# Feed-forward down products kept in PSUM: six banks that accumulate over all groups for the first 384 tokens, five rotating banks for the other 768

## The chip, the cores and the metric

The kernel runs on one core of a Trainium2 chip. The metric is device time in microseconds (us) of one execution. TensorE (PE) does the matrix products, VectorE (DVE), ScalarE (ACT) and GpSimd (POOL) the elementwise work, and SyncE (SP) issues the DMAs. Results of TensorE land in PSUM, which has eight banks of 128 partitions x 512 float32 values; DVE and ACT read it, POOL does not here.

## The reference

One layer of a hybrid backbone: 1024 sample tokens and 128 prompt tokens (nine tiles of 128) go through a mixer (mLSTM and attention), and then through a feed-forward part. The change touches the feed-forward part alone:

```
D_MODEL = 1024; D_FF = 4096; DEPTH = 1; ALPHA = 2 ** 0.25
x = layer_norm(ALPHA * x + g1 * mix, ln1_g, ln1_b)
h = x * (1 + sc2) + sh2
ff = jnp.square(jax.nn.relu(h @ w_up)) @ w_down
x = layer_norm(ALPHA * x + g2 * ff, ln2_g, ln2_b)
```

All of it is float32. The kernel splits each operand of a product in a high and a low part and takes three products (high x high, high x low, low x high): the helper `mm3`, lines 78 to 80.

## The kernel before

The 4096 hidden features are worked through in 16 groups (`NFB`) of 256. For each group there is an *up* product, the activation, and a *down* product that adds to the output of every token. The tokens are in two parts.

**First part, T0: tiles 0, 1, 2 (384 tokens).** `up_plain(fb)` loads two weight slots of `w_up` (`w_pair`: DMA to a `raw` buffer, high part on ACT in line 72, low part on DVE in line 73), runs 2 x 24 matmuls of 384 columns into banks of tag `u`, and takes relu (ACT), square (DVE) and the split to `ah`, `al`. `down(..., [fb], ...)` then does for three token tiles and two halves of 512 columns six matmuls into a bank of tag `d`, and DVE evicts it: a copy into `acc0` for group 0 (line 1168), an add to `acc0` for the later groups (line 1170). Groups 14 and 15 go together, twelve matmuls into one bank, and their eviction is part of the output stage: times gate `g2`, plus `acc0`, statistics of the layer norm (lines 1173 to 1175), then `finish` (lines 1139 to 1150). Before that, `residual` (lines 1131 to 1137) has multiplied `acc0` by the gate on POOL and has added ALPHA times the residual stream, read back from `x1d`.

While T0 runs, `act_forms` (lines 1112 to 1128) makes sums and differences of the activations of the other tokens: 32 operations on POOL, 16 additions and 16 subtractions, each subtraction followed by a split on ACT and DVE. The last of the nine token tiles is modulated and transposed late, between the two halves of `up_plain(1)` (`last_mod`, `modulate2`); the transposes use a pool of two banks, `ps3t`.

**Second part, T1: tiles 3 to 8 (768 tokens).** `up_halves` makes the up product with seven block products in place of eight (a Strassen-like scheme): 84 matmuls of 384 columns into three banks x, y and z. Its weights are sums of blocks, made by `up_forms` (POOL for the sums, line 1281, ACT and DVE for the splits) into three rotating `uf` slots. `down` runs twelve bank fills of six matmuls per group, each evicted by DVE.

PSUM before: pool `ps4` has three banks of tag `u` and three of tag `d`; `psx` has one bank each for x and y; z is taken from `u`.

The text of the kernel gives each operation a place, but the build orders the queue of each engine by planned times of its own, so an operation can stand ahead of ones that come earlier in the text.

Of the kernel before, what the change touches and what calls it, by code (L numbers as in the profile page):

```python
# [9 lines left out]
F32 = mybir.dt.float32  # L10
F32R = mybir.dt.float32r
# [25 lines left out]
def hybrid_step_kernel(  # L37
# [27 lines left out]
    def load(out, in_):  # L65
        nc.sync.dma_start(out=out, in_=in_)
# [892 lines left out]


    st3r = ctx.enter_context(ExitStack())
    st3 = ctx.enter_context(ExitStack())
    ps3t = pool(st3r, "ps3t", 2, space=PSUM, side="right")
    dp = pool(st3r, "dp", 1, side="right")
    ps3 = pool(st3, "ps3", 4, space=PSUM)
    xw = pool(st3, "xw", 4)
# [94 lines left out]

    x1s = {}

    def modulate2(s):
        if s // 3 not in h2T:
            h2T[s // 3] = t_alloc()
        hf = dt_([128, KT, 128], "m", 8)
        modulate(hf, s, x1s[s], sc2p, 24, t3)
# [32 lines left out]


    st4 = ctx.enter_context(ExitStack())
    ps4 = pool(st4, "ps4", 3, space=PSUM)
    tf = pool(st4, "tf", 1)
    fs = pool(st4, "fs", 1)
    wdv = kview(w_down)
    acts = {}
    for nm in ("s2", "s3", "a22"):
        acts[nm] = tuple(tf.tile([128, 4, TB], F32R, tag=nm + e, name="tf" + nm + e) for e in "hl")  # L1110

    def act_forms(mk):
        acts["a11"] = tuple(t[:, 0:4, :] for t in h2T[1])
# [41 lines left out]
    def down(mk, acc, toks, fbs, parts, ws, g2, l2, split_last):  # L1155
# [3 lines left out]
        for i, s in enumerate(toks):  # L1159
# [2 lines left out]
                st = mk([128, 2, 6], "bst", 2)  # L1162
            for half in range(2):
                cs = slice(512 * half, 512 * half + 512)
                g = ps4.tile([128, 512], F32, tag="d", name="d4")
                mm3(g[:], [((a[0][:, m, ts_], a[1][:, m, ts_]), (w[0][:, 0, cs], w[1][:, 0, cs])) for a, m, w in ws])
                if fbs[0] == 0:
                    nc.vector.tensor_copy(out=acc[:, i, cs], in_=g[:])
                elif not last:
                    nc.vector.tensor_tensor(out=acc[:, i, cs], in0=acc[:, i, cs], in1=g[:], op=ALU.add)  # L1170
                else:
                    tm = mk([128, 512], "x", 2)
                    nc.vector.tensor_tensor(out=tm[:], in0=g[:], in1=g2[0 if s < NS else 1][:, cs], op=ALU.mult)
                    nc.vector.tensor_tensor(out=acc[:, i, cs], in0=acc[:, i, cs], in1=tm[:], op=ALU.add)
                    nc.vector.bn_stats(out=st[:, half, :], in_=acc[:, i, cs])
# [36 lines left out]
            modulate2(late_.pop())  # L1212

    a = up_plain(0, lambda: None)
    nxt = up_plain(1, last_mod)
    st3r.close()
    s4r = ctx.enter_context(ExitStack())
    psx = pool(s4r, "psx", 1, space=PSUM, side="right")
    s4b = ctx.enter_context(ExitStack())
    ar0 = pool(s4b, "ar0", 1, side="right")  # L1220
    acc0 = ar0.tile([128, 3, D], F32, name="acc0")
    s4t = ctx.enter_context(ExitStack())
    tt4 = pool(s4t, "tt4", 1, side="right")
    forms = act_forms(lambda shape, tag: tt4.tile(list(shape), F32, tag=tag, name=tag))
# [2 lines left out]
        next(forms, None)  # L1227
        next(forms, None)

    T0 = (0, 1, 2)  # L1230
    for fb in range(NFB - 3):
        down(fat, acc0, T0, [fb], [a], down_w([fb]), None, None, False)
        a, nxt = nxt, up_plain(fb + 2, some_forms)
    for _ in forms:
        pass
# [10 lines left out]
    load_l2((l2a[:, 0, :], l2a[:, 1, :]))  # L1246
    todo = list(T0)

    def some():
        for _ in range(2):  # L1250
            if todo:
                s = todo.pop(0)
                residual(fft, acc0[:, s, :], s, g2a[:])

    down(fat, acc0, T0, [NFB - 3], [a], down_w([NFB - 3]), None, None, False)
    a, nxt = nxt, up_plain(NFB - 1, some)


    wuv = kview(w_up)
# [6 lines left out]
    def up_forms(fb):  # L1266
        raw = []
        for kh in range(2):
            t = rp.tile([128, 1024], F32, tag="raw", name="raw")[:].rearrange("p (k n) -> p k n", n=256)
            load(t, wuv[:, 4 * kh:4 * kh + 4, 256 * fb:256 * fb + 256])  # L1270
            raw.append(t)
        a11, a21 = raw[0][:, :, 0:128], raw[0][:, :, 128:256]
        a12, a22 = raw[1][:, :, 0:128], raw[1][:, :, 128:256]
        if fb:
            tmp = [wp.tile([128, 1024], F32R, tag="w" + e, name="wt" + e)[:] for e in "hl"]
        else:
            tmp = [fft([128, 1024], "wt", 2, F32R)[:] for e in range(2)]
# [26 lines left out]
        gen = up_forms(fb)  # L1304
        return gen, [next(gen) for _ in range(3)]

    ws = down_w([NFB - 2, NFB - 1])
    pre = up_begin(0)
    down(fft, acc0, T0, [NFB - 2, NFB - 1], [a, nxt], ws, [g2a], (l2a[:, 0, :], l2a[:, 1, :]), False)
    s4f.close()  # L1310
    s4b.close()
    s4a.close()
    fp = pool(st4, "fp", 1)
    aa = [fp.tile([128, 2, 768], F32R, tag="aa" + e, name="aa" + e) for e in "hl"]
    aa = ((aa[0][:], aa[1][:]), (ab[:, 0:2, :], ab[:, 2:4, :]))
    ar = pool(s4r, "ar", 1, side="right")
    acc = ar.tile([128, 6, D], F32, name="acc")

    def ft(shape, tag, bufs=1, ty=F32):
# [10 lines left out]
    def up_halves(pre, a, each):  # L1330
# [123 lines left out]
```

## Time and profile before

| | |
|---|---|
| time, median of 3 runs (lowest to highest) | 2518.7 us (2515.26 to 2519.15) |
| profiled execution, its own time | 2508.51 us |
| its span, first to last instruction | 2506.7 us |
| mean granted clock of TensorE, of full speed | 0.983 |
| TensorE busy | 2377.3 us, 95% of the span |
| DVE / ACT / POOL busy | 1553.9 / 991.4 / 489.4 us |
| T0 with the late token tile | about 1649 to 1945 us of the span |
| T1 | about 1945 to 2507 us |

The profiled execution took 2508.51 us, 1.8 us more than its span and 10.2 us less than the median of the three timed runs. A busy engine here is one with an instruction in progress; matmuls overlap, so the pace of TensorE is read from the starts of its instructions and not from their durations.

### The profile page before, as it was taken

The page shows a single profiled execution, that of the slowest core. Times are in us where ns is not written, and L with a number is a line of the kernel's source. Part 1 is how long each engine was busy: PE and PEld are TensorE (multiplying, and loading weights), DVE is VectorE, ACT ScalarE, POOL GpSimd, SP SyncE. Part 2 cuts the span into 40 slices and gives each one's busy share as a digit, 9 for nine tenths or more (in the row PEclk, how much of TensorE's full clock was granted, in tenths as well). Part 3 has the DMA queues.
Part 4 walks back from the last instruction along what each step waited for, and adds up shares of the span by engine and source line. Part 5 has one row for each costly group of instructions (what it writes and reads, how often), then busy time and mean ns, then how long its engine had stood idle before and what let it go on. Part 6 is the DMA issues. An engine that isn't in the chain of part 4 may idle for free.

```text
span 2506.7 us, 36075 instructions
## 1 busy us (share of the span) xinstructions
PE 2377.3 (95%) x13293; PEld 2136.6 (85%) x13293; DVE 1553.9 (62%) x2785; ACT 991.4 (40%) x2100; POOL 489.4 (20%) x635
## 2 busy tenths in 40 slices
PE   7999999999999899899999999997999899999996
PEld 4878887788999899889999999886998788888875
DVE  5645636646654554487885255777666766666678
ACT  3323423435433233276665242233333444433332
POOL 1001101102110010244441000343002422221143
PEclk9999999999999999999999999998999999999998
DMA  8275456445655643310004464233343221211223
GB/s 267 83 204 156 146 116 200 138 136 138 193 162 148 192 144 81 87 64 16 16 16 164 163 188 163 105 125 121 124 135 126 101 68 59 68 62 65 68 76 110
DMA packets 234544, 300.46 MB, mean 120 GB/s; under 512 B 24992, under 2 KB 175600, under 8 KB 234368
## 3 DMA queue, kind: packets, MB, share of 16 engines
q1 hardware_dynamic: 234368, 298.16, 38.7%
q8 instruction: 105, 1.72, 0.3%
q14 instruction: 71, 0.58, 0.1%
HBM read 232.88 MB, written 65.21 MB: 119 GB/s over the span
## 4 chain that ended last, share of the span: by engine, by line
PE 71%; DMA 9%; DVE 9%; POOL 4%; ACT 3%; issue 2%; SPq 0%; DVEq 0%; ACTq 0%; POOLq 0%
PE g L78 12%; PE g L80 12%; PE g L79 12%; PE d L78 3%; PE d L79 3%; PE d L80 3%; PE psy L1350 3%; PE t L872 2%; DMA raw<-in_w_down_dram 2%; DMA raw<-in_w_up_dram 2%; PE u L78 2%; PE u L79 2%; PE u L80 2%; POOL wth L1281 1%; DVE wl L73 1%
## 5 line engine op out<-in xcount | busy, mean ns | idle before, releaser
L78 PE MATMUL g<-th,wh 128*128 128x384 f32 x1088 | 373.2, 343 | 7.4 <-DVE fm L248 7.4
L80 PE MATMUL g<-th,wl 128*128 128x384 f32 x1088 | 367.7, 338 | 0.0
L79 PE MATMUL g<-tl,wh 128*128 128x384 f32 x1088 | 366.1, 337 | 0.0
L72 ACT ACTIVATE wh<-raw 128x1024 fp32r<-128x1024 f32 x180 | 188.8, 1058 | 258.9 <-DMA raw<-in_w_down_dram 87.3
L73 DVE TENSOR_TENSOR wl<-raw,wh 128x1024 fp32r<-128x1024 f32 x180 | 224.5, 1254 | 76.0 <-ACT wh L72 75.0
L78 PE MATMUL g<-wh,th 128*128 128x512 f32 x600 | 241.1, 402 | 0.9 <-ACT xq L643 0.8
L80 PE MATMUL g<-wh,tl 128*128 128x512 f32 x600 | 236.4, 394 | 0.0
L79 PE MATMUL g<-wl,th 128*128 128x512 f32 x600 | 236.0, 394 | 0.0
L78 PEld LDWEIGHTS g<-th,wh 128*128 128x128 f32 x1088 | 205.9, 189 | 16.2 <-DVE fm L248 7.7
L79 PEld LDWEIGHTS g<-tl,wh 128*128 128x128 f32 x1088 | 206.1, 189 | 0.1
L80 PEld LDWEIGHTS g<-th,wl 128*128 128x128 f32 x1088 | 205.7, 189 | 0.4 <-issue 0.4
L1170 DVE TENSOR_TENSOR acc<-acc,d 128x512 f32<-128x512 f32 x234 | 156.4, 683 | 67.2 <-PE d L80 67.2
L78 PEld LDWEIGHTS g<-wh,th 128*128 128x128 f32 x600 | 113.1, 188 | 26.3 <-issue 3.8
L80 PEld LDWEIGHTS g<-wh,tl 128*128 128x128 f32 x600 | 113.1, 189 | 23.5
L79 PEld LDWEIGHTS g<-wl,th 128*128 128x128 f32 x600 | 113.4, 189 | 20.3 <-DVE wl L73 0.4
L72 ACT ACTIVATE ph<-t 128x384 fp32r<-128x384 f32 x192 | 91.0, 493 | 70.6 <-PE t L872 70.2
L248 DVE COPY fm<-g 128x384 f32<-128x384 f32 x96 | 53.2, 555 | 99.6 <-PE g L80 99.3
L73 DVE TENSOR_TENSOR pl<-t,ph 128x384 fp32r<-128x384 f32 x192 | 104.8, 549 | 9.1 <-ACT ph L72 7.1
L872 PE MATMUL t<-ident,pe 128*128 128x128 f32 x576 | 96.2, 276 | 6.5 <-DVE pl L73 5.5
L78 PE MATMUL d<-wh,ah 128*128 128x512 f32 x192 | 77.2, 402 | 23.1 <-DVE acc L1170 16.5
L861 POOL TENSOR_SCALAR pe<-pe,rs 128x1152 f32<-128x1152 f32 x64 | 78.8, 1230 | 54.9 <-DVE rs L860 27.0
L78 PE MATMUL d<-wh,ab 128*128 128x512 f32 x192 | 77.6, 404 | 10.5 <-DVE acc L1170 9.5
(384 smaller groups left out, 5990.9 us busy)
## 6 DMA issues: line engine op xcount, KB each, us to landing
raw<-in_w_up_dram SPq DMA_DIRECT2D x64, 512.0 KB
raw<-in_w_down_dram SPq DMA_DIRECT2D x64, 512.0 KB
raw<-in_w_in_dram SPq DMA_DIRECT2D x44, 512.0 KB
kvt<-kvd SPq DMA_DIRECT2D x64, 257.0 KB
raw<-in_w_mod_dram SPq DMA_DIRECT2D x32, 512.0 KB
kvd<-kvs SPq DMA_DIRECT2D x36, 257.0 KB
uw<-ud SPq DMA_DIRECT2D x72, 128.0 KB
bs<-st SPq DMA_DIRECT2D x32, 258.0 KB
```

What stands on the lines that cost most here:

```text
L72: nc.scalar.activation(out=hi, in_=src, func=AF.Copy)
L73: nc.vector.tensor_tensor(out=lo, in0=src, in1=f(hi), op=ALU.subtract)
L78: nc.tensor.matmul(out, lhsT=ah, rhs=bh, start=start and i == 0, stop=False)
L79: nc.tensor.matmul(out, lhsT=ah, rhs=bl, start=False, stop=False)
L80: nc.tensor.matmul(out, lhsT=al, rhs=bh, start=False, stop=stop and i == n - 1)
L248: nc.vector.tensor_copy(out=st[:], in_=g[:, 0:TB])
L861: nc.gpsimd.tensor_scalar(pe[:], pe[:], rs[:, 0:1], 1.0, ALU.mult, ALU.mult)
L872: nc.tensor.transpose(pt[:, k, :], pexp[u][:, kt * 128:kt * 128 + 128], ident[:])
L1170: nc.vector.tensor_tensor(out=acc[:, i, cs], in0=acc[:, i, cs], in1=g[:], op=ALU.add)
L1281: nc.gpsimd.tensor_tensor(out=tmp[i], in0=x, in1=y, op=op)
L1350: nc.tensor.matmul(o, lhsT=x[:, k, :], rhs=y[:, k, :], start=fresh and k == 0 and i == 0, stop=k == 3 and i == 2, skip_group_check=True)
```

## The change

- T0 has six banks of its own (`psa`, tags a00 to a21), one for each token tile and half. `down_bank` adds all 16 groups in place: the first matmul of group 0 starts the sum, the last of group 15 ends it. The copies and adds to `acc0` are gone, and `acc0` with them.
- `residual` is gone for T0. The output stage `out0` runs inside `down_bank` of group 15, after each token tile: gate times bank, plus ALPHA times the residual stream, statistics, `finish`. The loads from `x1d` move into it, two buffers of 512 columns.
- Groups 14 and 15 of T0 are two separate down products.
- `ps4` keeps two `u` banks in place of three. `ps3t` is closed after `up_plain(0)`, and the late token tile is transposed after all of `up_plain(1)`, into `u` banks.
- T1: x and y come from the two `u` banks; a new pool `psd` has one z bank and five `d` banks in place of three. It lies where the six banks of T0 were.
- Buffers: the forms of the activations (`tf`) move from the left to the right side of SBUF; the raw weights of the first T1 group get a place of their own (`fft`, two buffers) in place of the shared `raw` buffers, and the sums made of them go to the shared weight slots `wp` in place of a place of their own. The accumulator of T1 moves to the left side.

```diff
-    ps4 = pool(st4, "ps4", 3, space=PSUM)
-    tf = pool(st4, "tf", 1)
+    ps4 = pool(st4, "ps4", 2, space=PSUM)
...
-                g = ps4.tile([128, 512], F32, tag="d", name="d4")
+                g = psd.tile([128, 512], F32, tag="d", bufs=5, name="d4")
...
     a = up_plain(0, lambda: None)
-    nxt = up_plain(1, last_mod)
+    st3t.close()
+    s4p = ctx.enter_context(ExitStack())
+    psa = pool(s4p, "psa", 1, space=PSUM, side="right")
+    dacc = [[psa.tile([128, 512], F32, tag=f"a{i}{h}", name=f"pa{i}{h}") for h in range(2)] for i in range(3)]
+    T0 = (0, 1, 2)
+
+    def down_bank(fb, a, ws, each):
+        for i in range(3):
+            ts_ = slice(128 * i, 128 * i + 128)
+            for half in range(2):
+                cs = slice(512 * half, 512 * half + 512)
+                mm3(dacc[i][half][:], [((a[0][:, m, ts_], a[1][:, m, ts_]), (w[0][:, 0, cs], w[1][:, 0, cs]))
+                                       for m, w in enumerate(ws)], fb == 0, fb == NFB - 1)
+            if each:
+                each(i)
+
+    nxt = up_plain(1, lambda: None)
+    modulate2(SORD[-1], lambda shape: ps4.tile(list(shape), F32, tag="u", name="u4"))
     st3r.close()
...
-    for fb in range(NFB - 3):
-        down(fat, acc0, T0, [fb], [a], down_w([fb]), None, None, False)
+    for fb in range(NFB - 2):
+        down_bank(fb, a, down_w([fb]), None)
         a, nxt = nxt, up_plain(fb + 2, some_forms)
...
-            t = rp.tile([128, 1024], F32, tag="raw", name="raw")[:].rearrange("p (k n) -> p k n", n=256)
+            t = rp.tile([128, 1024], F32, tag="raw", name="raw") if fb else fft([128, 1024], "raw", 2)
+            t = t[:].rearrange("p (k n) -> p k n", n=256)
...
+    def out0(s):
+        y = fft([128, D], "y0", 3)
+        st = fft([128, 2, 6], "bst", 2)
+        for half in range(2):
+            cs = slice(512 * half, 512 * half + 512)
+            x1 = fft([128, 512], "x", 2)
+            load(x1[:], x1d[s][:, cs])
+            nc.vector.tensor_tensor(out=y[:, cs], in0=dacc[s][half][:], in1=g2a[:, cs], op=ALU.mult)
+            nc.vector.scalar_tensor_tensor(out=y[:, cs], in0=x1[:], scalar=ALPHA, in1=y[:, cs], op0=ALU.mult, op1=ALU.add)
+            nc.vector.bn_stats(out=st[:, half, :], in_=y[:, cs])
+        finish(fft, y, s, l2a, *ln_stats(st, fft), 1)
+
+    ws = [down_w([fb]) for fb in (NFB - 2, NFB - 1)]
     pre = up_begin(0)
-    down(fft, acc0, T0, [NFB - 2, NFB - 1], [a, nxt], ws, [g2a], (l2a[:, 0, :], l2a[:, 1, :]), False)
+    down_bank(NFB - 2, a, ws[0], None)
+    down_bank(NFB - 1, nxt, ws[1], out0)
     s4f.close()
-    s4b.close()
     s4a.close()
+    s4p.close()
+    psd = pool(s4r, "psd", 1, space=PSUM, side="right")
...
-                bank[BANK[j]] = (ps4.tile([128, 512], F32, tag="u", name="u4") if BANK[j] == "z" else
-                                 psx.tile([128, 512], F32, tag=BANK[j], name="ps" + BANK[j]))
+                bank[BANK[j]] = (psd.tile([128, 512], F32, tag="z", name="pz") if BANK[j] == "z" else
+                                 ps4.tile([128, 512], F32, tag="u", name="u4"))
```

## Rows read from the trace of the kernel before

**Rows 1.** The page: the span, and busy time of the engines.
```profile
span 2506.7 us, 36075 instructions
PE 2377.3 (95%) x13293; PEld 2136.6 (85%) x13293; DVE 1553.9 (62%) x2785; ACT 991.4 (40%) x2100; POOL 489.4 (20%) x635
```
**Rows 2.** Busy time by stretch: length, PE, PEld, DVE, ACT, POOL, clock, DMA share, GB/s.
```profile
1649.00:1720.00 71.00, 50.41 (x251) 45.39 (x250) 56.65 (x70) 29.06 (x49) 45.51 (x35) 0.86 0.35 111
1720.00:1920.00 200.00, 200.00 (x1018) 182.52 (x1017) 129.88 (x170) 73.17 (x97) 7.53 (x3) 1.00 0.41 132
1920.00:1988.70 68.70, 54.97 (x257) 49.41 (x256) 49.78 (x67) 27.02 (x46) 25.61 (x20) 0.90 0.34 115
1988.70:2424.00 435.30, 418.18 (x2061) 368.76 (x2059) 285.62 (x388) 174.01 (x310) 96.93 (x70) 1.00 0.21 67
2424.00:2507.00 83.00, 61.42 (x272) 51.46 (x270) 67.22 (x95) 19.21 (x28) 35.72 (x24) 0.89 0.29 102
```
**Rows 3.** TensorE's waits, 1988.7 to 2424 us: total, times, longest.
```profile
PE d L78 <- DVE acc L1170: 14.3, 17, 1.8
PE d L78 <- DVE acc L1168: 1.9, 2, 1.3
```
**Rows 4.** Timeline of TensorE in one T1 group: start, duration, instruction, idle time before.
```profile
2059.75 0.39 PE L80 MATMUL d<-wh,aal 128*128 128x512 f32 x1
2061.08 0.50 PE L78 MATMUL d<-wh,aah 128*128 128x512 f32 x1 [0.94 <-DVE acc L1170]
```
**Rows 5.** Timeline of DVE in the same group.
```profile
2058.50 1.92 DVE L73 TENSOR_TENSOR uf<-wth,uf 128x512 fp32r<-128x512 f32 x2
2060.35 0.67 DVE L1170 TENSOR_TENSOR acc<-acc,d 128x512 f32<-128x512 f32 x1
...
2067.26 0.69 DVE L1170 TENSOR_TENSOR acc<-acc,d 128x512 f32<-128x512 f32 x1 [0.67 <-PE d L80]
2068.63 0.69 DVE L1170 TENSOR_TENSOR acc<-acc,d 128x512 f32<-128x512 f32 x1 [0.67 <-PE d L80]
```
**Rows 6.** The chain that ended last: first up block of two T1 groups.
```profile
2041.43 2.10 PE psx L1350 x12
...
2401.22 2.10 PE psx L1350 x12
```
**Rows 7.** Timeline of TensorE at the start of T0.
```profile
1675.11 0.50 PE L78 MATMUL d<-wh,ah 128*128 128x512 f32 x1 [4.13 <-DVE acc L1168]
...
1709.72 0.80 PE L78 MATMUL d<-wh,ah 128*128 128x512 f32 x1 [16.15 <-DVE acc L1170]
...
1724.28 0.39 PE L78 MATMUL d<-wh,ah 128*128 128x512 f32 x1
```
**Rows 8.** Timeline of POOL: first and last of the 32 form operations.
```profile
1672.17 1.87 POOL L1121 TENSOR_TENSOR va<-th,tl 128x384 f32<-128x384 f32 x1 [12.80 <-issue]
...
1713.24 1.02 POOL L1127 TENSOR_TENSOR va<-va,vs 128x384 f32<-128x384 f32 x1
```
**Rows 9.** Timeline of ACT: weight splits among and behind the forms.
```profile
1708.38 1.05 ACT L72 ACTIVATE wh<-raw 128x1024 fp32r<-128x1024 f32 x1
...
1715.50 2.01 ACT L72 ACTIVATE wh<-raw 128x1024 fp32r<-128x1024 f32 x2 [0.68 <-PE d L80]
```
**Rows 10.** Timeline of TensorE at the hand-over from T0 to T1.
```profile
1926.91 0.50 PE L78 MATMUL d<-wh,ah 128*128 128x512 f32 x1 [2.45 <-ACT wh L72]
...
1958.66 0.69 PE L1350 MATMUL psy<-tfs3h,uf 128*128 128x384 f32 x1 [7.05 <-DVE u L1339]
```
**Rows 11.** Timeline of SP's queue ahead of the last T0 weights.
```profile
1914.20 6.68 SPq L66 DMA_DIRECT2D x<-x1d  x3
```
**Rows 12.** The chain that ended last, at the hand-over.
```profile
1930.42 4.30 DMA raw<-in_w_up_dram
...
1939.83 1.22 DVE uf L73
```
**Rows 13.** Instructions on tile `d`: count, least/median/most ns, first and last start.
```profile
L1170 DVE TENSOR_TENSOR acc<-acc,d x234: 673/683/690, 1709.0 to 2438.6; 128x512 f32<-128x512 f32 x117
```

More of the change, by code (lines that the diff above doesn't have):

```diff
@@ L961, in hybrid_step_kernel @@
     st3r = ctx.enter_context(ExitStack())
+    st3t = ctx.enter_context(ExitStack())
     st3 = ctx.enter_context(ExitStack())
-    ps3t = pool(st3r, "ps3t", 2, space=PSUM, side="right")
+    ps3t = pool(st3t, "ps3t", 2, space=PSUM, side="right")
     dp = pool(st3r, "dp", 1, side="right")
@@ L1062, in hybrid_step_kernel, with modulate2 @@
     x1s = {}
-    def modulate2(s):
+    def modulate2(s, tt=None):
         if s // 3 not in h2T:
@@ L1067, in modulate2 @@
         hf = dt_([128, KT, 128], "m", 8)
-        modulate(hf, s, x1s[s], sc2p, 24, t3)
+        modulate(hf, s, x1s[s], sc2p, 24, tt or t3)
         o = (s % 3) * 128
@@ L1108, in hybrid_step_kernel @@
     acts = {}
-    for nm in ("s2", "s3", "a22"):
-        acts[nm] = tuple(tf.tile([128, 4, TB], F32R, tag=nm + e, name="tf" + nm + e) for e in "hl")
     def act_forms(mk):
@@ L1214, in hybrid_step_kernel @@
     a = up_plain(0, lambda: None)
-    nxt = up_plain(1, last_mod)
+    st3t.close()
[14 more added lines that the diff above has]
+    modulate2(SORD[-1], lambda shape: ps4.tile(list(shape), F32, tag="u", name="u4"))
     st3r.close()
     s4r = ctx.enter_context(ExitStack())
[L1218 to L1221, printed above, removed]
+    tf = pool(s4r, "tf", 1, side="right")
+    for nm in ("s2", "s3", "a22"):
+        acts[nm] = tuple(tf.tile([128, 4, TB], F32R, tag=nm + e, name="tf" + nm + e) for e in "hl")
     s4t = ctx.enter_context(ExitStack())
@@ L1228, in some_forms @@
         next(forms, None)
-    T0 = (0, 1, 2)
-    for fb in range(NFB - 3):
-        down(fat, acc0, T0, [fb], [a], down_w([fb]), None, None, False)
+    for fb in range(NFB - 2):
+        down_bank(fb, a, down_w([fb]), None)
         a, nxt = nxt, up_plain(fb + 2, some_forms)
@@ L1245, in hybrid_step_kernel @@
     l2a = fft([128, 2, D], "l2a")
[L1246 to L1256, printed above, removed]
+    l2a = (l2a[:, 0, :], l2a[:, 1, :])
+    load_l2(l2a)
     wuv = kview(w_up)
@@ L1273, in up_forms @@
         a12, a22 = raw[1][:, :, 0:128], raw[1][:, :, 128:256]
[L1274 to L1277, printed above, removed]
+        tmp = [wp.tile([128, 1024], F32R, tag="w" + e, name="wt" + e)[:] for e in "hl"]
         tmp = [f(t[:, 512 * i:512 * i + 512]).rearrange("p (k n) -> p k n", n=128) for t in tmp for i in range(2)]
@@ L1305, in up_begin @@
         return gen, [next(gen) for _ in range(3)]
-    ws = down_w([NFB - 2, NFB - 1])
+    def out0(s):
[10 more added lines that the diff above has]
+    ws = [down_w([fb]) for fb in (NFB - 2, NFB - 1)]
     pre = up_begin(0)
-    down(fft, acc0, T0, [NFB - 2, NFB - 1], [a, nxt], ws, [g2a], (l2a[:, 0, :], l2a[:, 1, :]), False)
+    down_bank(NFB - 2, a, ws[0], None)
+    down_bank(NFB - 1, nxt, ws[1], out0)
     s4f.close()
-    s4b.close()
     s4a.close()
+    s4p.close()
+    psd = pool(s4r, "psd", 1, space=PSUM, side="right")
     fp = pool(st4, "fp", 1)
@@ L1315, in hybrid_step_kernel @@
     aa = ((aa[0][:], aa[1][:]), (ab[:, 0:2, :], ab[:, 2:4, :]))
-    ar = pool(s4r, "ar", 1, side="right")
+    ar = pool(st4, "ar", 1)
     acc = ar.tile([128, 6, D], F32, name="acc")
```

## The prediction

> **What bounds the kernel now.** I read the page first: TensorE is busy for 95% of the span [rows 1], so a change that removes no matmul can only win back time in which TensorE stands still, and work taken from DVE is worth nothing by itself. The change removes many DVE instructions and no matmul. The question is therefore where TensorE waits for the things that the change touches.
>
> The second view is the busy time by stretch, cut at the places where the work changes [rows 2]. From 1720 to 1920 us, most of T0, TensorE is busy for 200.0 of 200.0 us at the full clock. The copies and adds to `acc0` that the change removes there are wholly hidden. What can be won lies in four other places: the start of T0 (20.6 us idle of 71.0, clock 0.86), the hand-over to T1 (13.7 idle of 68.7, clock 0.90), the long stretch of T1 (17.1 idle of 435.3, clock 1.00), and the end (21.6 idle of 83.0).
>
> The third view is the waits of TensorE in T1 [rows 3]: 16.2 us in all, every one a down product that waits for DVE to evict a bank. The timelines of one group show how [rows 4, 5]. Three bank fills go at full pace, the fourth starts 1.33 us after the instruction before it in place of 0.23. DVE had been held in its in-order queue by two splits of the next weights, 2058.50 to 2060.4, and only then added the bank that had been ready since about 2057.2 (the third fill ends 0.23 us after 2059.75, the first two fills of 1.37 us before that). Later in the group DVE itself waits 0.67 us for each fill, so it has the throughput; it is only late at the start of each down product.
>
> **The change part by part.**
>
> *Five `d` banks in T1.* A fill is six matmuls; DVE, when it waits for fills, starts every 1.37 us [rows 5]. Twelve fills take 16.4 us, and the seven up blocks 7 x 2.10 = 14.7 us [rows 6], together 31.1. The first up blocks of two groups eleven apart stand at 2041.43 and 2401.22, so a group takes 32.7 us. The 1.6 us between are the wait and its restart (the first matmul behind a wait takes 0.50 in place of 0.39 [rows 4], and shorter waits follow). With 14 groups that is 22.5 us; the waits alone are 16.2. With five banks TensorE meets a bank that DVE has not read only if DVE is four fills late, 5.5 us. In the group shown it is late by some 3.2 us (2060.35 less 2057.2), so all of it should vanish. I take 22 us; bounds 0 (the first rival) and 24 (22.5 and the 1.9 us of waits for the copies of group 0).
>
> The Trainium skill (page "TensorE: Matmul & The Clock Gate", section on HAM oscillation) speaks against this part: after a kernel's loop had been put in a better order, double-buffering in PSUM gave no further gain, 126.6 against 125.5 us. By that rule this term would be about nothing, by the rows here 22 us.
>
> z falls from three shared banks to one. Its next fill comes a whole group after its last read, so I cost that at nothing; x and y stay on one bank each. The adds themselves stay, at 683 ns each [rows 13].
>
> *The start of T0.* Two waits on `d` disappear, 4.13 and 16.15 us [rows 7]. But I do not count 20 us. The forms of the activations run on POOL back to back from 1672.17 to 1714.3, 32 operations in 42 us [rows 8], since the build has drawn them all together. ACT and DVE must split their results in order, and weight splits stand in the same queues: the second slot of the weights of up group 3 came at 1708.38, those of down group 2 at 1715.50 [rows 9]. Without the waits for banks TensorE would reach up group 3 at about 1694 (the second wait began at 1693.6, three fills of 1.37 us were left, and the first wait is gone too), and wait there for weights. What counts is when down group 2 can start, 1724.28 before [rows 7]. If the forms start at about 1674 (the late tile is transposed up to half an up product, 4.2 us, later, but DVE no longer has copies ahead of it), they end at 1716; the two splits on ACT and one on DVE (2.0 and about 1.2 us) let down group 2 start at about 1720, and the slow clock after a wait takes some 1 us. Gain 3. Bounds: the forms shift by the full 4.2 us and two more are lost as TensorE waits for a `u` bank for the transposes, so down group 2 starts at 1728: loss 4. Or the build puts the weight splits ahead of the last quarter of the forms, 10.5 us earlier: gain 12. The tiles of the forms lie elsewhere now, on memory that is read last at about 1672; the first is written later than that, so no wait.
>
> *Two `u` banks in T0, in place of three.* A bank is wanted again one up half and one down product later, over 8 us; ACT, which must read it, is busy for 73 of 200 us in the saturated stretch [rows 2]. Nothing, as long as ACT is not held up by forms.
>
> The Trainium skill (page "PSUM — Partial Sum Buffer", summary of rules) asks for PSUM to be emptied promptly, as it is small; six banks held for all of T0 are the opposite. By that rule the up products would lose; the 200.0 of 200.0 us say that there is room.
>
> *The hand-over.* Three things. First, the residual's loads of `x1d` held SP's queue for 6.68 us [rows 11] ahead of the weights of the last down products, and TensorE waited 2.45 us [rows 10]. Now the weights come first: 2.45 saved. Second, the raw weights of the first T1 group could only be loaded when a shared buffer came free, 1930.42 to 1934.72, and DVE was held until 1939.83 for the splits of their sums [rows 12] while its output stage waited behind. Now they are loaded early, and the sums wait for the end of down group 14. That group began at about 1923 (1926.91 less the wait and one fill) and takes six fills, 8.2 us, so the sums start at 1931 in place of 1934.9. DVE should pass the point of 1939.83 at about 1936 with two or three output operations of 0.68 us undone, and the sum for which TensorE waited until 1958.66 [rows 10] comes some 2 us earlier. TensorE will stand longer there (its own work ends sooner), but the end is set by DVE: the output stage has the same three operations for each half as before. So the first saving is not added to this one; both end in the same DVE queue. Third, the weights of the second T1 group are free to load earlier as well: 1 to 2 us. Gain 4. Bounds: both waits go entirely, 9.5; or the loads of `x1d`, which now sit inside the output stage with two buffers, hold DVE by the 6.68 us that they held SP: 2.5 - 6.7, loss 4.
>
> The z bank lies on one of the six that `out0` must read first; TensorE wants it two up blocks after T0's end, and waits there or one block later for DVE anyway.
>
> *The end.* The last down products of T1 are fills of twelve matmuls, slower than DVE's part, so the extra banks change little: 0, bounds 2 either way.
>
> *The sum.* 22 + 3 + 4 = 29 us. Against the profiled execution that is 2508.5 - 29 = 2479.5; the runs' median is 10.2 us above that execution, and on it I predict 2518.7 - 29 = 2489.7, put as 2490 us.
>
> **The rivals.** Times are on the scale of the median; 0.2% is 5 us.
>
> 1. *DVE's order holds T1, not the banks.* Splits of weights and forms stay ahead of the adds, and what TensorE gains in the down product it loses in the next up product. For it: DVE is 66% busy there [rows 2] and blocks in order. Against it: DVE waits for fills in the second half of every group [rows 5]. T1 then gives 5 in place of 22: 2507. The rule of double-buffering would give this too. Chance 0.12.
> 2. *The start of T0 opens as well*, because the forms fall behind the weight splits: 12 in place of 3, and the hand-over gives 8: about 2476. For it: the late tile is later by half an up product in the plan. Against: nothing but POOL's 42 us decides. Chance 0.12.
> 3. *The hand-over eats the gain.* `out0` waits for its loads in series with its stores in SP's queue; to bring the time near 2510 it would have to cost 16 us more than I allow, over twice what the loads cost in [rows 11]. Chance 0.07.
> 4. *Slower: the plan of T1 turns against TensorE.* With more banks the build may place adds later, so that the sums of the up blocks, for which TensorE waited 7.05 us at the hand-over [rows 10], come late in every group. It decides at 29 / 16 = 1.8 us for each group; at 3 us the time is 2518.7 + 16 x 3 - 29 = 2538. Against it: TensorE shows no such wait in the stretch now [rows 3]. Chance 0.07.
>
> My forecast holds 0.62, with its own range 2478 to 2502. The range that should hold 8 in 10 reaches into the second rival and most of the first: 2474 to 2508. Faster by over 0.2%: the forecast, the first two rivals but for 0.02, and a little of the third, 0.87; within 0.2%: 0.05; slower: 0.08.
>
> **What the profile after would show.** T1's period from up block to up block near 31.1 us, and no `d <- DVE` waits: the first term is right; a period above 32 makes it wrong. The wait at the start of T0 still there, but at weights or at a `u` bank in place of a `d` bank, with down group 2 starting 3 us earlier: the second. At the hand-over no wait for weights in the last down products, one longer wait at the fourth up block: the third. The prediction is wrong if up products in T1 begin to wait for DVE, or if a wait of over 25 us stands at either end of T0.

## The result, and the profile after

The changed kernel takes 2481.7 us (median of 4 runs, 2480.7 to 2482.2), the kernel before 2517.0 us beside it: a ratio of 0.9859, 95% interval 0.9842 to 0.9876, or 35 us. Predicted were 29 us and 2490 us, with 2478 to 2502 as the forecast's own range.

The head of the page, after, answers to [rows 1]:

```profile
PE 2371.1 (96%) x13293; PEld 2141.3 (86%) x13293; DVE 1492.7 (60%) x2695; ACT 989.7 (40%) x2100; POOL 481.6 (19%) x632
```

DVE lost 61 us of work, and TensorE has the same 13293 matmuls. To see where the time came from, both executions are cut at the same events: the first up matmul of T0, the first matmul of down group 2, the start of the last 72 down matmuls, T0's last matmul, the first down matmul of T1, the first matmul of T1's down group 13, the end. Before (length, then PE, PEld, DVE, ACT, POOL busy, clock, DMA share, GB/s):

```profile
1649.06:1724.28 75.22, 54.63 (x276) 49.61 (x274) 58.15 (x73) 31.14 (x52) 45.51 (x35) 0.86 0.38 120
1724.28:1922.90 198.62, 198.62 (x1009) 181.14 (x1009) 131.23 (x170) 71.08 (x94) 7.53 (x3) 1.00 0.40 128
1922.90:1945.20 22.30, 18.87 (x74) 14.56 (x74) 15.87 (x24) 5.44 (x8) 7.01 (x7) 0.92 0.41 129
1945.20:1989.00 43.80, 33.50 (x170) 32.25 (x169) 31.30 (x41) 21.88 (x38) 18.90 (x14) 0.88 0.31 108
1989.00:2415.60 426.60, 410.87 (x2029) 363.04 (x2028) 277.12 (x380) 168.97 (x301) 91.28 (x67) 1.00 0.21 67
2415.60:2506.70 91.10, 68.43 (x302) 56.87 (x300) 75.42 (x103) 23.95 (x37) 41.08 (x27) 0.90 0.28 98
```

After, the same six stretches:

```profile
1655.10:1728.50 73.40, 60.46 (x275) 54.34 (x273) 53.62 (x59) 29.88 (x51) 45.48 (x35) 0.84 0.37 121
1728.50:1927.10 198.60, 198.60 (x1010) 181.28 (x1009) 84.96 (x98) 74.00 (x98) 0.00 (x0) 1.00 0.43 136
1927.10:1943.50 16.40, 16.40 (x74) 13.56 (x74) 7.53 (x9) 3.75 (x6) 8.86 (x7) 1.00 0.21 64
1943.50:1986.40 42.90, 32.82 (x169) 31.67 (x168) 34.37 (x51) 21.96 (x40) 16.93 (x14) 0.88 0.40 132
1986.40:2389.20 402.80, 402.80 (x2031) 365.31 (x2030) 271.95 (x379) 167.90 (x301) 90.33 (x67) 1.00 0.22 70
2389.20:2479.60 90.40, 65.76 (x301) 54.48 (x299) 74.68 (x103) 23.68 (x36) 41.26 (x27) 0.93 0.28 99
```

Read the first number of each line against its partner: 1.8, 0.0, 5.9, 0.9, 23.8 and 0.7 us, together 33.1. The second line is the plainest lesson: DVE's work there fell from 131 to 85 us, and the stretch kept its length. The fifth is the large one: TensorE now works through all 402.8 us of T1. (The spans differ by only 27.1 us, since in this execution T0 began 6.0 us later, with the same instructions ahead of it but for one of POOL; more on that in the last section. Stretches are compared below, not spans.)

T1 in detail. The chain that ended last, first up blocks of two groups eleven apart, answers to [rows 6]:

```profile
2003.01 4.18 PE u L1366 x24
...
2343.79 4.18 PE u L1366 x24
```

340.78 / 11 = 30.98 us for a group, where 32.7 were needed before and 31.1 were predicted. DVE in one group and, in the last line, in a later one, for [rows 5]:

```profile
2051.06 1.93 DVE L73 TENSOR_TENSOR uf<-wth,uf 128x512 fp32r<-128x512 f32 x2
2052.91 0.68 DVE L1168 TENSOR_TENSOR acc<-acc,d 128x512 f32<-128x512 f32 x1
...
2054.96 1.23 DVE L73 TENSOR_TENSOR wl<-raw,wh 128x1024 fp32r<-128x1024 f32 x1 [0.31 <-ACT wh L72]
2056.10 3.08 DVE L1168 TENSOR_TENSOR acc<-acc,d 128x512 f32<-128x512 f32 x5
...
2119.27 4.49 DVE L1168 TENSOR_TENSOR acc<-acc,d 128x512 f32<-128x512 f32 x7
```

DVE is as late as it was: two splits, then the first add at 2052.91, though its bank was filled at about 2049.8 (the down product begins at 2048.4, a fill takes 1.37). At 2056.10 it takes up the third bank, filled at about 2052.5, and catches up with five adds in a row. In this group it lags by up to 3.6 us, and five banks hold that. In two of the 13 groups of the stretch it lags by more: in the first, whose evictions are the copies, by 4.7 us, and in the fifth by 4.9 us. The last line shows the fifth: its down product begins at 2110.30, its third bank is filled at about 2114.4 and taken up at 2119.27. That down product takes 16.7 us from its first to its last matmul, where the others behind the first take 16.4.

### The profile page after: what moved, and what is told of

It reads as the page before. It is cut to its first block, busy times and chain, and to the rows that moved or that the text cites. A ratio compares the mean times of both kernels' runs of the same rounds, so it can differ in the third digit from the quotient of the medians.

```text
span 2479.6 us, 35982 instructions
## 1 busy us (share of the span) xinstructions
PE 2371.1 (96%) x13293; PEld 2141.3 (86%) x13293; DVE 1492.7 (60%) x2695; ACT 989.7 (40%) x2100; POOL 481.6 (19%) x632
## 5 line engine op out<-in xcount | busy, mean ns | idle before, releaser
L72 ACT ACTIVATE wh<-raw 128x1024 fp32r<-128x1024 f32 x180 | 188.9, 1058 | 258.2 <-DMA raw<-in_w_down_dram 90.9
L80 PEld LDWEIGHTS g<-wh,tl 128*128 128x128 f32 x600 | 113.0, 188 | 23.3
L72 ACT ACTIVATE ph<-t 128x384 fp32r<-128x384 f32 x192 | 90.9, 493 | 70.9 <-PE t L872 70.4
L1168 DVE TENSOR_TENSOR acc<-acc,d 128x512 f32<-128x512 f32 x156 | 101.9, 681 | 28.5 <-PE d L80 28.4
L1283 POOL TENSOR_TENSOR wtl<-raw 128x512 f32<-128x512 f32 x16 | 20.9, 1304 | 438.3 <-PE pa L79 211.3
L78 PE MATMUL u<-th,wh 128*128 128x384 f32 x256 | 89.6, 350 | 10.9 <-ACT wh L72 7.2
L80 PE MATMUL u<-th,wl 128*128 128x384 f32 x256 | 89.0, 348 | 1.8 <-DVE wl L73 1.8
```

Of the source, the lines that this page charges most:

```text
L72: nc.scalar.activation(out=hi, in_=src, func=AF.Copy)
L78: nc.tensor.matmul(out, lhsT=ah, rhs=bh, start=start and i == 0, stop=False)
L80: nc.tensor.matmul(out, lhsT=al, rhs=bh, start=False, stop=stop and i == n - 1)
L1283: nc.gpsimd.tensor_tensor(out=tmp[i], in0=x, in1=y, op=op)
```

## The experiments

Times are medians; each ratio is against the kernel before on the same chip in the same set of runs (2511.8, 2509.1, 2514.1 and 2511.5 us in the four sets: e, r, f, g). The stretches are those of the tables above (start of T0, last down block, hand-over, T1, end); the middle of T0 is 198.6 us in all but e3, where it is 199.4. The sets ran on different chips, so times of different sets are compared by their ratios.

| kernel | us | ratio [95%] | start | block | hand-over | T1 | end |
|---|---|---|---|---|---|---|---|
| before | | 1 | 75.2 | 22.3 | 43.8 | 426.6 | 91.1 |
| after | 2481.7 | 0.9859 [0.9842, 0.9876] | 73.4 | 16.4 | 42.9 | 402.8 | 90.4 |
| e1 three `d` banks | 2503.7 | 0.9967 [0.9954, 0.9980] | 73.4 | 16.4 | 42.9 | 427.1 | 91.6 |
| e2 four `d` banks | 2483.1 | 0.9881 [0.9865, 0.9898] | 71.2 | 16.4 | 42.6 | 408.0 | 90.9 |
| e3 five banks alone | 2489.0 | 0.9907 [0.9892, 0.9922] | 75.1 | 23.3 | 43.1 | 402.9 | 90.3 |
| e4 forms drawn out | 2462.9 | 0.9805 [0.9790, 0.9820] | 55.1 | 16.3 | 42.9 | 404.1 | 90.6 |
| r1 raw weights shared | 2476.4 | 0.9867 [0.9852, 0.9881] | 73.2 | 16.4 | 43.0 | 403.4 | 91.7 |
| r2 placements as before | 2478.3 | 0.9871 [0.9856, 0.9886] | 73.3 | 16.4 | 42.6 | 403.5 | 91.1 |
| r3 sums in own tile | 2471.2 | 0.9847 [0.9832, 0.9862] | 71.3 | 16.4 | 36.9 | 402.5 | 90.1 |
| r4 loads into output tiles | 2476.6 | 0.9864 [0.9848, 0.9881] | 73.6 | 16.4 | 41.9 | 402.5 | 90.3 |
| f1 e4 + r3 + r4 | 2460.1 | 0.9787 [0.9772, 0.9802] | 57.3 | 16.4 | 38.5 | 404.2 | 92.0 |
| f2 after, again | 2479.1 | 0.9864 [0.9848, 0.9881] | 73.6 | 16.4 | 43.5 | 402.5 | 91.3 |
| g1 groups 14 and 15 joint | 2477.7 | 0.9861 [0.9844, 0.9877] | 71.1 | 16.7 | 43.4 | 402.6 | 90.7 |
| g2 e4 + r3 | 2457.7 | 0.9782 [0.9763, 0.9800] | 58.8 | 16.4 | 37.0 | 404.8 | 91.8 |

**The banks of T1 (e1, e2, e3).** e1 and e2 are the changed kernel with three and four `d` banks:

```diff
-                g = psd.tile([128, 512], F32, tag="d", bufs=5, name="d4")
+                g = psd.tile([128, 512], F32, tag="d", bufs=3, name="d4")
```

> The changed kernel with three d banks for tiles 3 to 8 in place of five; all else as changed. Theory (the banks hold the second part): the period from one first up block to the next goes back from 31.0 to 32.6 or 32.7 us, waits of the down products on DVE come back (about 16 us in all), time about 2505 us (2500 to 2509), so that what is left against the kernel before, some 10 to 14 us, is the part of the first tiles and the hand-over. Rival (the gain there comes from a lighter DVE or another order of the queues, not from the banks): period stays near 31, time 2481 to 2486.

> Four d banks in place of five. Theory: DVE reads the first fill of a group some 3 to 3.5 us late, four banks cover 3 x 1.37 = 4.1 us, so nearly all of the gain stays: waits on DVE under 3 us in all, time 2480 to 2485. Rival (each bank carries its share): half of the gain is lost, about 2493.

e3 is the kernel before with five `d` banks in T1 and nothing else of the change, but that x, y and z share the three `u` banks:

```diff
+    def d_bank(many):
+        turn[0] += 1
+        if many and turn[0] % 5 > 2:
+            return psx.tile([128, 512], F32, tag="e", bufs=2, name="d4")
+        return ps4.tile([128, 512], F32, tag="d", name="d4")
...
-                g = ps4.tile([128, 512], F32, tag="d", name="d4")
+                g = d_bank(len(toks) > 3)
...
-                bank[BANK[j]] = (ps4.tile([128, 512], F32, tag="u", name="u4") if BANK[j] == "z" else
-                                 psx.tile([128, 512], F32, tag=BANK[j], name="ps" + BANK[j]))
+                bank[BANK[j]] = ps4.tile([128, 512], F32, tag="u", name="u4")
```

> The kernel before, with five d banks for tiles 3 to 8 alone (three of the pool of the first part and two more; x, y and z in the three u banks); the first part keeps its accumulator and its evictions. Theory: the second part gains its 22 to 24 us and nothing else moves, time about 2493 us (2489 to 2498), period 31.0. Rival (the six accumulating banks are needed for it, since they change the order of the queues or free DVE): 2508 to 2517.

TensorE's waits in T1 of e1 (total, times, longest), which are those of [rows 3] again:

```profile
PE d L78 <- DVE acc L1168: 12.5, 14, 1.8
PE d L78 <- DVE acc L1166: 2.2, 2, 1.7
```

The same waits in T1 of e2, and T1 of e3 by busy time:

```profile
PE d L78 <- DVE acc L1166: 0.9, 2, 0.5
PE d L78 <- DVE acc L1168: 0.8, 2, 0.5
```

```profile
1993.20:2396.10 402.90, 402.82 (x2030) 365.20 (x2029) 274.91 (x380) 169.09 (x302) 91.40 (x67) 1.00 0.23 71
```

Three banks give 427 us with everything else changed; five give 403 with nothing else changed but the place of x, y and z; e1, which moves them too, keeps the old 427. The banks are the cause, for 23.7 to 24.3 us. Four give 408, so 5.2 us of the 23.8 are lost, between the theory (nearly none) and its rival (half). A bank is free only when its add ends, 0.68 us after DVE has taken it up: a lag of 3.4 to 3.6 us makes 4.1 to 4.3, about the 4.1 us (three fills of 1.37) that three spare banks cover. All four waits lie in the first and the fifth group, where the lag is longer; the other down products take 16.5 to 16.7 us in place of 16.4.

**The start of T0 (e4).** The changed kernel, with POOL's forms tied to the activations: before each two forms POOL copies one column of `r`, and they are issued behind that copy.

```diff
-    def some_forms():
-        next(forms, None)
-        next(forms, None)
+    def some_forms(r):
+        ins = nc.gpsimd.tensor_copy(out=mark[:], in_=r[:, 0:1]).ins
+        with tc.issue_after(ins):
+            next(forms, None)
+            next(forms, None)
...
```

> The changed kernel, with the forms of the activations held back: before every two of them POOL copies one column of the activation of that up half, so that they run over up groups 2 to 9 in place of all together. Theory (POOL's 42 us of forms in the same in-order queues as the weight splits bound the start of the first part): from its start to down group 2 the time falls from 73.4 to some 53 to 60 us, the waits of up group 3 for weights vanish, time 2463 to 2471. Rival (what bounds it is the arrival and the slots of the weights, or the two u banks): less than 5 us, 2477 to 2484.

The start and the middle of T0, after that edit:

```profile
1653.00:1708.10 55.10, 52.76 (x275) 49.17 (x274) 34.24 (x45) 23.50 (x37) 11.36 (x12) 0.97 0.45 143
1708.10:1906.70 198.60, 198.60 (x1011) 181.26 (x1010) 105.47 (x113) 81.08 (x112) 33.45 (x50) 1.00 0.45 141
```

POOL's work moves from the first line (45.5 us after, 11.4 here) to the second (0 after, 33.5 here), where TensorE does not notice it. The start shrinks by 18.3 us. So it was the forms, drawn together ahead of the weight splits, that kept the start long once the waits for banks were gone.

**The hand-over (r1 to r4).** r1 puts the raw weights of T1's first group back in the shared buffers; r2 does that and puts the sums back in a place of their own; r3 gives the sums a tile that nothing else waits on (and allocates the second activation tile behind them); r4 loads the residual into the output tiles.

```diff
r1
-            t = rp.tile([128, 1024], F32, tag="raw", name="raw") if fb else fft([128, 1024], "raw", 2)
+            t = rp.tile([128, 1024], F32, tag="raw", name="raw")
r2, beside that
-        tmp = [wp.tile([128, 1024], F32R, tag="w" + e, name="wt" + e)[:] for e in "hl"]
+        tmp = [(wp.tile([128, 1024], F32R, tag="w" + e, name="wt" + e) if fb else fft([128, 1024], "wt", 2, F32R))[:] for e in "hl"]
r3, where fb is 0
...
+            sums = tp.tile([128, 6, 512], F32R, tag="t", name="sums")[:].rearrange("p a n -> p (a n)")
+            tmp = [sums[:, 1024 * e:1024 * e + 1024] for e in range(2)]
...
r4
-            load(x1[:], x1d[s][:, cs])
-            nc.vector.tensor_tensor(out=y[:, cs], in0=dacc[s][half][:], in1=g2a[:, cs], op=ALU.mult)
+            load(y[:, cs], x1d[s][:, cs])
+            nc.vector.tensor_tensor(out=x1[:], in0=dacc[s][half][:], in1=g2a[:, cs], op=ALU.mult)
```

> The changed kernel, but the raw up weights of T1's first group go to the two shared raw buffers again, as before the change; the sums stay in the split weights' pool. Measured around the hand-over, from the start of T0's second down group to T1's first down product: before 264.7 us, after 257.9 us, a gain of 6.8. Theory A (the early raw load is what the hand-over gained by, since ACT's split of the second group's weights no longer waits for a raw buffer that group 0 holds): TensorE waits again in the hand-over, by 4 to 7 us; about 2486 us. Rival B (the gain comes from the down products that need no additions at the end of T0, not from the loads): same as the changed kernel, 2482 us.

> The changed kernel with the raw weights and the split sums of T1's first group both placed as before the change, all else of the change kept. Theory A (raw place matters, place of the sums costs some back): the sums no longer wait for the end of down 14, so 1 to 3 us better than the run with the raw weights alone moved back; about 2484 us. Rival C (both placements together are worth the whole 6.8 us of the hand-over): 2488 us. Rival B (placements are worth nothing): 2482 us.

> The changed kernel with POOL's split sums of T1's first group in a tile of their own, so that they don't wait for a split-weight buffer that is freed only at the end of T0's last down group. Theory D (that wait is what leaves TensorE's one wait of 7.5 us for the second group's up weights in the hand-over): the sums begin by about 1927 instead of 1934.6 us, the wait falls to about 3, and the time to about 2477 us. Rival E (the late weights are ACT's and DVE's own order of work, the sums are not in its chain): 2482 us, with the wait of 7 us still there.

> The changed kernel with the residual of the first output loaded straight into the output tiles, so that all six loads are issued early and only the product goes to the two x buffers. Theory F (after the change DVE waits only 0.9 us for these loads in the hand-over, so they are out of the way): 2481 us, within 2 us of the changed kernel. Rival G (the loads still hold DVE's first output and with it the second group's weights): 2476 us.

r1 and r2 are misses for the placements: the hand-over stays at 43.0 and 42.6 us. Inside it something moves, though. From the sum block that waited 7.05 us in [rows 10] to the first down product of T1, r1 and then the changed kernel:

```profile
1951.78:1980.70 28.92, 26.32 (x128) 24.88 (x129) 20.54 (x26) 16.79 (x32) 12.44 (x10) 0.89 0.45 146
```

```profile
1959.73:1986.40 26.67, 24.77 (x128) 24.45 (x129) 19.02 (x26) 17.36 (x33) 8.97 (x7) 0.91 0.46 153
```

The early raw weights are worth 2.3 us there, and from T0's end up to that block they cost 2.1 (16.2 us against 14.1 in r1). r2 repeats both (28.7 and 13.9 us). r4's hand-over is 1.0 us shorter: the loads were nearly out of the way, as theory F has it. Its time is the figure of rival G, 2476, but the kernel before was 7.9 us faster in that set than beside the changed kernel; by its ratio r4 is the changed kernel's equal.

r3 is the hit: 6.0 us. Its POOL and DVE, and then the changed kernel's:

```profile
1922.58 3.63 POOL L1286 TENSOR_TENSOR sums<-raw 128x512 f32<-128x512 f32 x2 [202.83 <-PE u L79]
...
1932.27 0.69 DVE L1319 TENSOR_TENSOR y<-pa,g 128x512 f32<-128x512 f32 x1
```

```profile
1934.64 1.29 POOL L1283 TENSOR_TENSOR wtl<-raw 128x512 f32<-128x512 f32 x1 [211.32 <-PE pa L79]
...
1937.87 1.10 DVE L73 TENSOR_TENSOR uf<-wth,uf 128x512 fp32r<-128x512 f32 x1 [6.76 <-ACT uf L72]
1938.89 0.68 DVE L1316 TENSOR_TENSOR y<-pa,g 128x512 f32<-128x512 f32 x1
```

After the change POOL may write the sums only when TensorE has read down group 14's weights out of the shared slot. DVE stands 6.76 us in its queue for the first split of a sum, with the output stage behind it. In r3 POOL starts the sums as the last down block begins, 16.3 us ahead of T0's end and not 8.9, and DVE starts the output stage 6.6 us before T0's end, not 4.6 us (1938.9 less 1932.27, and 1943.5 less 1938.89), and no split of a sum interrupts it.

**The last down products of T0 (g1).** The changed kernel with groups 14 and 15 filled together, twelve matmuls into a bank:

```diff
-    down_bank(NFB - 2, a, ws[0], None)
-    down_bank(NFB - 1, nxt, ws[1], out0)
+    for i in T0:
+        ts_ = slice(128 * i, 128 * i + 128)
+        for half in range(2):
+            cs = slice(512 * half, 512 * half + 512)
+            mm3(dacc[i][half][:], [((v[0][:, m, ts_], v[1][:, m, ts_]), (w[0][:, 0, cs], w[1][:, 0, cs]))
+                                   for v, wg in ((a, ws[0]), (nxt, ws[1])) for m, w in enumerate(wg)], False, True)
+        out0(i)
```

> The changed kernel, but the last two down products of T0 go together again, twelve matmuls into a bank at a time, as before the change; the loads stay in the changed order. The block of 72 down products at the end of T0 took 22.3 us before and takes 16.4 after. Theory H (the 5.9 us are SP's order: the weights of group 15 now come ahead of the residual's loads, and ACT splits them without waiting for a DMA): the block stays at 16.4 to 17 us though each bank needs the second group's weights from its seventh matmul on. Rival I (they are the separate order, which needs group 15's weights only 8.2 us later): 19 to 22 us. In both, the sums of T1's first group wait for a weight slot that is freed some 8 us later, so the hand-over grows from 43 to about 48 us, and the whole is about 5 us slower than the changed kernel by H, 8 to 11 by I.

The block took 16.7 us, so rival I falls: the block did not gain by the order of the products. That leaves theory H, the order of the loads, for which the waits in the kernel before speak too (next section); no run puts the loads back in their old order. The expected loss behind the block did not come: the hand-over stays at 43.4. The sums come 9 us later in g1 (POOL starts them 0.3 us behind T0's end, after the change 8.9 ahead of it), but the first token tile is ready sooner, and DVE starts the output stage 12.1 us ahead of T0's end, where it was 4.6.

**Together (f1, f2, g2).** f1 has the edits of e4, r3 and r4, g2 those of e4 and r3, f2 none.

> The changed kernel with three edits together: POOL's forms drawn out over the groups (by 19 us faster in the first set of runs), the sums of T1's first group in a tile of their own (hand-over 36.9 instead of 43.0 us), and the residual loads straight into the output tiles (hand-over shorter by 1.1 us). If the three gains lie in different stages and add up: start of T0 about 54 us to the second down group, hand-over about 36, T1 unchanged at 403; some 25 us less than the changed kernel, so about 2457 us where the changed kernel takes 2481. Rival: the two hand-over edits remove the same wait, and the time is about 2460.

> The changed kernel itself, once more beside the one with three edits, as the measure for it on the same chip: 0.984 to 0.988 of the kernel before, with the stages as in its first profile (73.5 us from the start of T0 to its second down group, 215 to the end of T0, 43 in the hand-over, 403 in T1), whatever the stretch ahead of T0 takes.

> The changed kernel with POOL's forms drawn out and the sums in a tile of their own, without the third edit (the loads straight into the output tiles). With all three the start of T0 took 57.3 us (55.1 with the forms alone), the hand-over 38.5 (36.9 with the sums alone) and the end 92.0 (90.6 with the forms alone). Theory J (the third edit costs what was missing to the sum of the gains): 55 us, 37 us and 90.6, some 4 us less than with all three, about 0.977 of the kernel before. Rival K (the forms drawn out and the sums' tile stand in each other's way): as with all three, 0.9787.

Both combinations beat both kernels: 0.9787 and 0.9782 of the time before. f1 is 19 us below the changed kernel beside it (f2), where 25 were expected and 21 by the rival. In the profiles the gains do not add up in full. The hand-over keeps its 6 us in g2 (37.0) and is 1.5 us longer with the third edit, which is the part of theory J that came true; but the start of T0 is 3.7 us longer in g2 than in e4, so the third edit is not to blame for that. By their times J and K cannot be told apart: g2's interval holds both.

ACT and TensorE at the start of T0 in g2 show most of it:

```profile
1676.66 1.06 ACT L72 ACTIVATE wh<-raw 128x1024 fp32r<-128x1024 f32 x1 [3.26 <-DMA raw<-in_w_up_dram]
```

```profile
1678.15 0.66 PE L195 MATMUL u<-ident,m 128*128 128x128 f32 x4 [2.20 <-ACT r L1200]
```

ACT stands 3.26 us at a load of up weights that is issued as early as in e4 but lands later. The read of a `u` bank stands behind it in ACT's queue, and the transposes of the late token tile wait 2.20 us for that bank. f1 has the same wait of 2.21 us, e4 has none, and r1, with neither of the two edits, has one of 1.87: so it does not take these edits to bring the wait about, and why the load lands later stays open. The other 1.5 us of g2 are the clock: in this stretch the granted clock is 0.94, in e4 and f1 0.97, and TensorE is busy for 54.3 us in place of 52.8. The profiled executions of f1 and g2 took 2462.6 and 2462.7 us, 2.5 and 5.0 above the medians, so the stretches show a little more loss than the medians hold. The end, 1.2 us longer in g2 than in e4, varies between 90.1 and 92.0 us over all kernels with five banks.

## Why the prediction was right

**T1, predicted 22, measured 23.8.** The mechanism is the one given: DVE late at the start of each down product by some 3.2 us (3.1 to 3.6 in the group shown), bridged by banks. The size comes out near by two slips that nearly cancel: the sum counted 14 groups, and the stretch holds 13; and the value taken left out the two waits for the copies of group 0 [rows 3]. Twelve groups gain some 1.7 us each (32.7 less 30.98) and the first 3.2. The margin of the five banks is also smaller than the one group suggested: DVE's lag of 4.9 us in the fifth group and 0.7 for the add come to about the 5.5 us that the prediction gives them. Rival 1 is dead: no up product of T1 waits for DVE, TensorE is busy for 402.8 of 402.8 us, and e3 has the whole gain alone. Rival 4 falls with it. The Trainium skill's remark (page "TensorE: Matmul & The Clock Gate", section on HAM oscillation) that double-buffering in PSUM gave no further gain does not carry over: from three banks to five it is 24 us of 427 here, as the consumer of the banks is late in bursts while its mean load is 64% (DVE in T1 of e1: 275.0 of 427.1 us).

**The start of T0, predicted 3, measured 1.8.** Not the 20 us of the two waits that went. TensorE after, for [rows 7]:

```profile
1671.84 0.69 PE L78 MATMUL u<-th,wh 128*128 128x384 f32 x1 [3.67 <-ACT r L1200]
...
1711.23 0.69 PE L78 MATMUL u<-th,wh 128*128 128x384 f32 x1 [5.87 <-ACT wh L72]
```

The wait stands at the weights of up group 3, as predicted, and POOL and ACT give the reason, for [rows 8, 9]:

```profile
1685.40 2.33 POOL L1119 TENSOR_TENSOR va<-th,tl 128x384 f32<-128x384 f32 x2 [18.36 <-DVE tl L73]
...
1722.12 1.21 POOL L1125 TENSOR_TENSOR va<-va,vs 128x384 f32<-128x384 f32 x1
```

```profile
1717.02 1.04 ACT L72 ACTIVATE wh<-raw 128x1024 fp32r<-128x1024 f32 x1
...
1724.20 1.99 ACT L72 ACTIVATE wh<-raw 128x1024 fp32r<-128x1024 f32 x2
```

Counted from T0's first matmul the forms end at 68.2 us, against 65.2 before and 66.9 predicted; ACT's split of down group 2's weights follows at once, and the down product 5.2 us behind the last form, where the prediction allowed 4 and some 1 for the slow clock. That the forms end so near to the forecast is partly luck: POOL makes three of the 32 before the late token tile is there and the other 29 only from 1685.40 on, 30.3 us after T0's first matmul, where the prediction had about 25 for all. What it costed at nothing is the row at 1671.84: with two `u` banks TensorE waited 3.67 us for ACT to read one. That happens once, in the second up product; in the middle of T0 two are enough, and the six banks that are held all through cost nothing (198.6 of 198.6 us busy). By the rule weighed there (the Trainium skill, page "PSUM — Partial Sum Buffer", summary of rules) the up products should lose: true of that one wait, not of the stretch.

The measured 1.8 us is one of two sizes. In e2, r3 and g1 the order of the instructions up to down group 2 is that of the changed kernel, and so are the waits, to 0.4 us; yet their start takes 71.1 to 71.3 us, a gain of 4. The granted clock there is 0.90, and 0.84 in the profile of the changed kernel (last section). The predicted 3 us lie between. The lower bound that the prediction gives (1728, loss 4) does not follow from its terms: 1714.3 + 4.2 + 2 + 3.2 + 1 is 1724.7, a loss of 0.4.

Rival 2 (the start opens as well) did not come by itself, and e4 shows what it would have been: 20 us against the kernel before (75.2 to 55.1), not the 12 that were put down as the bound. The prediction's reason against it, POOL's 42 us of forms, is what e4 takes away.

**The hand-over, predicted 4, measured 6.8, by another sum.** The prediction counted about 2 us at the sum block, 1 to 2 behind it, and left the 2.45 us of late weights out, since both would end in DVE's queue. The rows: the last down block is 5.9 us shorter, TensorE then stands 2.8 us longer up to the sum block (16.2 against 13.5 us), and the rest is 3.7 shorter (26.7 against 30.3): 5.9 - 2.8 + 3.7 = 6.8. Three things in that were mis-sized.

First, the late weights cost 5.9 us and not 2.45. Busy time of the kernel before from that block's start, around the wait of [rows 10] and behind it:

```profile
1922.90:1926.90 4.00, 1.56 (x7) 0.95 (x6) 2.60 (x5) 1.58 (x2) 0.00 (x0) 1.00 0.87 288
1926.90:1928.30 1.40, 0.50 (x1) 0.19 (x1) 1.36 (x2) 0.23 (x1) 0.00 (x0) 0.99 0.24 97
1928.30:1931.80 3.50, 3.48 (x8) 2.78 (x9) 2.05 (x3) 1.73 (x3) 0.00 (x0) 0.51 0.56 166
```

The first line holds the wait of 2.45 us. In the second TensorE gets one matmul in and waits 0.91 us more, now for the low part of the weights. In the third the granted clock is 0.51, the 1.2 GHz level: eight matmuls take 3.5 us, which at 0.23 us each take 1.8. ACT's splits of these weights, in the kernel before, waited for their DMAs:

```profile
1925.80 1.06 ACT L72 ACTIVATE wh<-raw 128x1024 fp32r<-128x1024 f32 x1 [0.77 <-DMA raw<-in_w_down_dram]
1928.08 1.06 ACT L72 ACTIVATE wh<-raw 128x1024 fp32r<-128x1024 f32 x1 [1.22 <-DMA raw<-in_w_down_dram]
```

After the change ACT splits the same weights at 1925.10 and 1927.18, as soon as TensorE has freed the slots, and the block runs at full pace; in g1 it does so with the old order of the products. In SP's queue after, the weights stand ahead of the residual, for [rows 11]:

```profile
1910.90 11.24 SPq L66 DMA_DIRECT2D raw<-in_w_down_dram  x4
...
1943.67 6.81 SPq L66 DMA_DIRECT2D x<-x1d  x4
```

Second, "not added" was half wrong: TensorE stands longer, as the prediction says, but gives back 2.8 of the 5.9 us, not all. DVE's output stage also starts from the last down products, and these end earlier. Third, the second group gains 3.7 us and not 1 to 2; r1 shows that 2.3 of them come from the early raw weights, which is the mechanism given, a little above its bound. r1 shows too that the same early loads cost 2.1 us ahead of the sum block, so that the placements as a whole are worth about nothing. The total of 4 thus stands near 6.8 partly by luck: of its parts one (the placements) nets to zero, and what was left out of it (the loads' order) brings nearly 6.

TensorE's one long wait there, predicted at the sum block (1959.73 after), stands 2.4 us ahead of it and at ACT's split:

```profile
1957.38 0.69 PE L1366 MATMUL u<-th,uf 128*128 128x384 f32 x1 [7.48 <-ACT uf L72]
```

r3 names its cause: the sums that wait for down group 14 to end. The prediction had this step and its time (the sums some 4 us earlier than before), but not that a tile of their own would have given 6 us more. Rival 3 is out: DVE waited 0.88 us for the loads of `x1d` in the output stage, and in r4, where they are issued early, the hand-over is 1.0 us shorter.

**The end, predicted 0, measured 0.7**, within its bound of 2. The reason given leaves out the one group of six-matmul fills that lies in this stretch: its down product takes 18.8 us after and 22.4 before, and most of that is given back in the up product behind it, where TensorE now waits 1.5 us for DVE and 0.5 for ACT.

**The time, predicted 2489.7, measured 2481.7.** Of the 8.0 us the stretches hold 4.1 (33.1 against 29), and the kernel before ran 1.7 us faster beside the changed one than in the runs shown ahead; the other 2.2 lie ahead of T0 or between executions, and no row shows where.

## What to carry to other kernels

Look at how late the engine that empties PSUM is in its worst burst, not at its mean load: banks that cover the burst turn the whole wait into work. Here the lag is 3.4 to 3.6 us in most groups and 4.9 in the worst, the add that frees the bank takes 0.7 more, and a spare bank covers a fill of 1.37 us: four spare banks (5.5 us) were enough, with three (4.1 us) 5 of the 24 us were lost. Where a wait goes, ask in the same engine queues what is late next, and what drew it together; the start of T0 gave 2 us of its 20 until the forms on POOL were spread out, and then 18 more. Price a late operand by the wait, the waits for its other parts and the slow matmuls behind it, which came to more than twice the wait here.

## What the runs showed of the hardware that was not expected

The stretch ahead of T0 has the same instructions in both profiles of the changed kernel, and T0 began at 1655.1 us in one execution and at 1651.6 in the other (f2); in the 14 profiles together it began between 1647.7 (r2) and 1655.1. Differences of a few us between two spans say little here. The later stretches of these two executions agree within 0.6 us, but for the end (90.4 and 91.3).

The start of T0 repeats less well from kernel to kernel, and the granted clock is what differs. This is e2, to be read against the first line after (73.40 us, TensorE busy 60.46, clock 0.84):

```profile
1653.90:1725.10 71.20, 57.77 (x275) 51.80 (x274) 53.04 (x58) 29.53 (x50) 45.51 (x35) 0.90 0.37 119
```

The instructions and their order are the same, TensorE's waits agree within 0.4 us, and the stretch is 2.2 us shorter with 2.7 us less of busy time. e2, r3 and g1 show 0.90 (71.1 to 71.3 us), the changed kernel in both its profiles, and e1, 0.84 (73.4 to 73.6 us). What decided between the two no run shows. A difference of 2 us in a stretch in which TensorE waits says nothing, then, before the clocks have been compared.

Behind the waits of 2.45 and 0.91 us in the last down block before, TensorE's granted clock was 0.51 for a stretch of 3.5 us and then 1.00 again, as in the rows above; behind the wait of 0.94 us in T1 [rows 4] one matmul took 0.50 in place of 0.39 us, and the whole of T1 shows a clock of 1.00.
